# Five blocks of an output projection with other operand layouts: interleaved weights, 512 and 256 columns, another order of the three products, three PSUM banks

## The chip, the cores and the metric

The kernel runs on one core of one Trainium2 chip. The metric is the device time of one execution in microseconds (us); smaller is better. A profile is taken of one execution by the hardware profiler. The engines are called PE (TensorE, the matrix unit), PEld (its weight loads, which run under its matmuls), DVE (VectorE), ACT (ScalarE), POOL (GpSimd) and SP (SyncE, which here only starts transfers). SBUF is the working memory on the chip, PSUM the memory that matmuls write their sums to.

## The reference: what is computed

One layer of a streaming encoder, for 256 frames of a new stream and 64 frames of a running one, which share the weights. The kernel joins the two groups to T = 320 columns. Cut to what matters here:

```
proj = rmsnorm(x) @ w_in                    # q, k, v, u, v_s, gates
a  = stick_breaking_attention(q, k, v, cache)
bb = spatial_gate(gelu(u), rmsnorm(gelu(v_s)))
merged = g_a * (a @ w_branch_a) + g_b * (bb @ w_branch_b)
h = x + merged @ w_out                      # the output projection
gu = rmsnorm(h) @ w_gate_up
h = h + (silu(gu[:F]) * gu[F:]) @ w_down
y = rmsnorm(h)
```

The change concerns the line with `w_out`: a product of a 320 x 2048 activation with a 2048 x 2048 matrix, all in 32-bit floating point.

## The kernel before

Features lie on the 128 partitions, the 320 frames on the free dimension. A weight matrix is cut into blocks: one block makes 128 output features and has K / 128 tiles of 128 x 128 weights. For the output projection there are 16 blocks (`for m in range(KD)`, L660 to L666), and each sums over 16 values of k.

**Split operands.** TensorE's format fp32r keeps fewer bits than float32. So every operand is split into a high part (rounded to fp32r) and a low part (what the rounding left), and a product is three matmuls: high weights x high activation, high weights x low activation, low weights x high activation (`product`, L80 to L85). Each of them brings its 128 x 128 weights as a load of its own. For one block of the output projection these are 16 x 3 = 48 matmuls of 320 columns, all into one PSUM bank.

**Weights.** `weights` (L68 to L78) brings 8 tiles of weights, half a block, as one transfer of 512 KB on SP's queue into `raw` (three buffers), casts them on ACT to `wh` (L75) and subtracts on DVE to get `wl` (L76). `wh` and `wl` have four buffers each, so a cast for the half that comes four later waits until TensorE has used up the old one.

**The block.** `block` (L87 to L97) takes a PSUM accumulator `acc` (L45, three buffers of 512 columns, which is one bank), runs the two halves and returns the first 320 columns. The caller evicts: in the output projection DVE adds the residual x, which it has loaded to `xr` (L662), to the accumulator and writes h (L664); ACT and DVE then make the split, gain-scaled copy of h that the feed-forward part takes as its activation (L123, L124), and a sum of squares of h is kept (L197 on ACT, L198 mostly on POOL).

**The activation of the output projection** is `merged`, 16 pairs of tiles `mh` and `ml` (L651 to L655), 128 x 320 each, written at the end of each merge step.

**Order.** A scheduler decides the order of instructions on each engine, apart from those marked to be kept in program order. Small pieces of work of the attention are hung in between blocks by a counter of half blocks (`tick`); none falls into the output projection.

Other matmuls that the prediction uses as measures: L243 (the first blocks, fp32r, two heads at once in two PSUM banks), L416, L488 and L604 (attention and spatial gate, plain float32, 128 or 64 columns), L418 (attention, fp32r, 256 columns).

Of the kernel before, what the change touches and what calls it, by code (L numbers as in the profile page):

```python
# [8 lines left out]
F32 = mybir.dt.float32  # L9
F32R = mybir.dt.float32r  # L10
AF = mybir.ActivationFunctionType
ALU = mybir.AluOpType

P = 128
TP = 256
TS = 64
T = TP + TS
D = 2048
KD = D // P
H = 8  # L20
HALF = 8
# [12 lines left out]
def stream_step(ctx: ExitStack, tc: tile.TileContext, xT, w_in, w_a, w_b, w_out, w_gu, w_down,  # L34
                gains, ws_t, bs, ck_t, cv, y_t, k_t, v_t, sv_t):
    nc = tc.nc
    pool = lambda name, bufs=1, **kw: ctx.enter_context(tc.tile_pool(name=name, bufs=bufs, **kw))
    const = pool("const")
    wraw = pool("wraw", 3)
    wsplit = pool("wsplit", 4)  # L40
# [4 lines left out]
    def acc():  # L45
        return psum.tile([P, 512], F32, tag="acc", bufs=3, name="acc")

    def aux():
        return psum.tile([P, 512], F32, tag="aux", bufs=4, name="aux")

    def aux1():
        return psum.tile([P, 512], F32, tag="aux1", bufs=1, name="aux1")
# [9 lines left out]
    def tick():  # L62
        state["tick"] += 1
        for fn, a in later.pop(state["tick"], ()):
            fn(*a)


    def weights(src, n, view=lambda t: t):  # L68
        raw = wraw.tile([P, HALF * P], F32, tag="raw", name="raw")
        d = nc.sync.dma_start(out=view(raw[:, : n * P]), in_=src)  # L70
        if state["tick"] < 4:
            tc.keep_in_program_order(d)
        wh = wsplit.tile([P, HALF * P], F32R, tag="wh", name="wh")
        wl = wsplit.tile([P, HALF * P], F32R, tag="wl", name="wl")
        nc.scalar.copy(out=wh[:, : n * P], in_=raw[:, : n * P])  # L75
        nc.vector.tensor_tensor(out=wl[:, : n * P], in0=raw[:, : n * P],  # L76
                                in1=wh[:, : n * P].bitcast(F32), op=ALU.subtract)
        return wh, wl  # L78

    def product(ps, w, j, x, first, last):  # L80
        wh, wl = w
        a, b = wh[:, j * P : (j + 1) * P], wl[:, j * P : (j + 1) * P]
        nc.tensor.matmul(ps[:, :T], a, x[0], start=first, stop=False)  # L83
        nc.tensor.matmul(ps[:, :T], a, x[1], start=False, stop=False)  # L84
        nc.tensor.matmul(ps[:, :T], b, x[0], start=False, stop=last)  # L85

    def block(src, act):  # L87

        ps = acc()
        nk = len(act)  # L90
        for k0 in range(0, nk, HALF):
            n = min(HALF, nk - k0)
            w = weights(src[:, k0 * P : (k0 + n) * P], n)
            for j in range(n):
                product(ps, w, j, act[k0 + j], k0 + j == 0, k0 + j == nk - 1)
            tick()
        return ps[:, :T]  # L97

    def slot(tag):
        return big.tile([P, T], F32R, tag=tag, bufs=32, name=tag)  # L100
# [20 lines left out]
    def gained(tag, src, gain):  # L121
        hi, lo = slot(tag), slot(tag)
        nc.scalar.activation(out=hi, in_=src, func=AF.Copy, scale=gain)  # L123
        nc.vector.scalar_tensor_tensor(out=lo, in0=src, scalar=gain, in1=hi.bitcast(F32),  # L124
                                       op0=ALU.mult, op1=ALU.subtract)
        return hi, lo

    def t320(tag, bufs=2, dt=F32):
        return tmp.tile([P, T], dt, tag=tag, bufs=bufs, name=tag)
# [76 lines left out]
    first = [[acc(), acc()], [aux(), aux()], [aux(), aux()]]  # L206
# [340 lines left out]
    for h in range(2, H):  # L547
        if h % 2 == 0:
            att_new(h // 2)
            at(state["tick"] + 6, att_keys, h // 2)  # L550
            at(state["tick"] + 9, att_past, h // 2)
        for name, b in (("k", 1), ("q", 0), ("v", 2)):
            head_out(name, block(w_in[b * H + h], xs), h)
        if h % 2:
            att_parts(h // 2)
            attend(h // 2, state["tick"])
# [4 lines left out]
    for g in range(H):  # L561
        ps = block(w_in[4 * H + g], xs)
        t = t320("ev")
        nc.vector.tensor_tensor(out=t, in0=ps, in1=got["rx"], op=ALU.mult)
        nc.scalar.activation(out=vs[g], in_=t, func=AF.Gelu_apprx_tanh)
        sq.add(vs[g])
# [57 lines left out]
    for g in range(H):  # L624
        ps = block(w_in[3 * H + g], xs)
        t = t320("ev")
        nc.vector.tensor_tensor(out=t, in0=ps, in1=got["rx"], op=ALU.mult)
        nc.scalar.activation(out=us[g], in_=t, func=AF.Gelu_apprx_tanh)
# [3 lines left out]
    merged = []  # L632
    for m in range(KD):
        gate = []
        for i in range(2):
            ps = block(w_in[5 * H + i * KD + m], xs)
            t = t320("ev")
            nc.vector.tensor_tensor(out=t, in0=ps, in1=got["rx"], op=ALU.mult)
            gt = t320(f"gate{i}", 1)
            nc.scalar.activation(out=gt, in_=t, func=AF.Sigmoid, bias=b_gate[:, i * KD + m : i * KD + m + 1])  # L640
            gate.append(gt)
        if m == 0:
            att_ctx.close()
            mpool = mctx.enter_context(tc.tile_pool(name="merged", bufs=1))
        ps = block(w_a[m], [aT[h] for h in range(H)])
        t = t320("mg", 1)
        nc.vector.tensor_tensor(out=t, in0=ps, in1=gate[0], op=ALU.mult)
        ps = block(w_b[m], [bT[g] for g in range(H)])
        nc.vector.tensor_tensor(out=gate[1], in0=ps, in1=gate[1], op=ALU.mult)
        nc.vector.tensor_tensor(out=t, in0=t, in1=gate[1], op=ALU.add)  # L650
        hi = mpool.tile([P, T], F32R, tag="C", bufs=32, name="mh")  # L651
        lo = mpool.tile([P, T], F32R, tag="C", bufs=32, name="ml")
        nc.scalar.copy(out=hi, in_=t)
        nc.vector.tensor_tensor(out=lo, in0=t, in1=hi.bitcast(F32), op=ALU.subtract)
        merged.append((hi, lo))  # L655


    (hs, ypair), hg = halves(KD, "h"), []
# [1 line left out]
    for m in range(KD):  # L660
        x = t320("xr")
        tc.keep_in_program_order(nc.sync.dma_start(out=x, in_=xT[:, m, :]))  # L662
        ps = block(w_out[m], merged)
        nc.vector.tensor_tensor(out=hs[m], in0=ps, in1=x, op=ALU.add)  # L664
        hg.append(gained("A", hs[m], g_ffn[:, m : m + 1]))
        sq.add(hs[m], nc.vector if m == KD - 1 else None)  # L666
# [6 lines left out]
    last = const.tile([P, T], F32, name="last")  # L673
# [3 lines left out]
    for s0, n in SLICES:  # L677
        act = []
# [17 lines left out]
        for m in range(KD):  # L696
            ps = block(w_down[m][:, s0 * P : (s0 + n) * P], act)
# [20 lines left out]
    ps, cols = aux1(), aux()  # L718
    keep(nc.tensor.matmul(cols[:, 1:2], mones, tiny, start=True, stop=False, skip_group_check=True))
    for i, t in enumerate((sqf.total, last)):  # L720
        keep(nc.tensor.matmul(ps[:, inner], mones, t[:, inner], start=i == 0, stop=i == 1))  # L721
        for c, r in enumerate(COLS):
            keep(nc.tensor.matmul(cols[0 : r.stop - r.start, c : c + 1], t[:, r], mones[:, 0:1], start=False,
                                  stop=i == 1, skip_group_check=True))
# [4 lines left out]
    x, e = root[:, inner], half[:, inner]  # L729
# [10 lines left out]
    for c, r in enumerate(COLS):  # L740
        keep(nc.tensor.matmul(far[:, r], col[:, c : c + 1].to_broadcast([P, P]), ident[:, 0 : r.stop - r.start],
                              start=c == 0, stop=c == 1, skip_group_check=True))
# [83 lines left out]
```

## Time and profile before

| what | value |
|---|---|
| time, median of 3 runs | 1701.74 us (1701.65 to 1701.96) |
| span of the profiled execution | 1700.0 us |
| DVE busy | 881.0 us |
| ACT busy | 673.2 us |
| POOL busy | 58.4 us |
| DMA, mean over the span | 158 GB/s |
| output projection, first to last eviction | 653.0 to 758.6 us |
| mean granted TensorE clock | 0.998 |

The profiled execution's own time is its span, from the first to the last instruction; the runs are timed from outside and come out 1.74 us above it. A row of a group reads: line, engine, operation, output <- inputs, shape, count, busy time and mean length of one in ns, then the idle time of the engine ahead of it and what ended it. A row of the order in time begins with its start and its length in us. A row of the chain of work that ended last has start, length, engine, what is written, line and count. TensorE's ends are modelled by the profiler, so that neighbouring matmuls overlap in the rows; their starts are what can be measured.

### The profile page before, as it was taken

Reading aid. Unit: us, or ns where it says so; the run is one execution under the profiler, and the core shown is the slowest. Engines: PE = TensorE matmul, PEld = TensorE weight load, DVE = VectorE, ACT = ScalarE, POOL = GpSimd, SP = SyncE. Lnnn points to the kernel's source line nnn. Section 1 sums busy time; section 2 is a strip of 40 time slices with the busy share of each in tenths; the row PEclk is TensorE's granted clock in tenths of the full one; section 3 lists DMA queues with packets and bytes.
Section 4 is the critical chain, followed back from the end, with each engine's and each line's share of the span. In section 5 each row is a group of like instructions: output and inputs, shape, how many; then the busy total and the mean of one; then the engine's idle time right before and its main releaser. Section 6 shows DMA issues by size and latency. Waiting matters only on the chain.

```text
span 1700.0 us, 27477 instructions
## 1 busy us (share of the span) xinstructions
PE 1690.0 (99%) x11550; PEld 1689.2 (99%) x11550; DVE 881.0 (52%) x1150; ACT 673.2 (40%) x885; POOL 58.4 (3%) x81
## 2 busy tenths in 40 slices
PE   9999999999999999999999999999999999999997
PEld 9999999999999999999999999999999999999997
DVE  6677656544444445555444444444444444444455
ACT  6655545433333333443333332333333323333342
POOL 0300021000000000110000000000000000000000
PEclk9999999999999999999999999999999999999999
DMA  6676556544444455554444455444444554444453
GB/s 249 195 219 173 172 168 173 147 151 152 150 150 151 150 156 165 173 164 149 150 149 150 150 152 150 151 151 149 150 149 149 149 149 150 150 152 149 132 150 124
DMA packets 100507, 268.30 MB, mean 158 GB/s; under 512 B 28992, under 2 KB 35392, under 8 KB 100384
## 3 DMA queue, kind: packets, MB, share of 16 engines
q1 hardware_dynamic: 97936, 261.36, 49.8%
q0 software_dynamic: 1312, 3.80, 0.7%
q8 instruction: 90, 1.47, 0.4%
q10 hardware_dynamic: 1136, 1.39, 0.2%
q14 instruction: 33, 0.27, 0.0%
HBM read 256.03 MB, written 5.51 MB: 154 GB/s over the span
## 4 chain that ended last, share of the span: by engine, by line
PE 99%; DVE 0%; DMA 0%; ACT 0%; DVEq 0%; issue 0%
PE acc L84 32%; PE acc L83 32%; PE acc L85 32%; PE aux L243 2%; PE acc L243 1%; PE aux L488 1%; DVE h L749 0%; PE aux L604 0%; DMA gain<-gains 0%; PE aux L418 0%; PE aux L421 0%; PE aux L416 0%; PE aux L602 0%; PE aux L721 0%; ACT A L123 0%; ACT wh L233 0%
## 5 line engine op out<-in xcount | busy, mean ns | idle before, releaser
L75 ACT CAST wh<-raw 128x1024 fp32r<-128x1024 f32 x468 | 484.4, 1036 | 922.8 <-PE acc L84 746.6
L76 DVE TENSOR_TENSOR wl<-raw,wh 128x1024 fp32r<-128x1024 f32 x468 | 564.8, 1207 | 476.0 <-ACT wh L75 475.3
L83 PE MATMUL acc<-A,wh 128*128 128x320 f32 x2464 | 762.0, 309 | 0.0
L85 PE MATMUL acc<-A,wl 128*128 128x320 f32 x2464 | 761.4, 309 | 0.0
L84 PE MATMUL acc<-A,wh 128*128 128x320 f32 x2464 | 761.4, 309 | 0.0
L83 PEld LDWEIGHTS acc<-A,wh 128*128 128x128 f32 x2464 | 462.5, 188 | 0.0
L84 PEld LDWEIGHTS acc<-A,wh 128*128 128x128 f32 x2464 | 462.5, 188 | 0.0
L85 PEld LDWEIGHTS acc<-A,wl 128*128 128x128 f32 x2464 | 462.5, 188 | 0.0
L83 PE MATMUL acc<-B,wh 128*128 128x320 f32 x960 | 296.6, 309 | 0.0
L84 PE MATMUL acc<-B,wh 128*128 128x320 f32 x960 | 296.6, 309 | 0.0
L85 PE MATMUL acc<-B,wl 128*128 128x320 f32 x960 | 296.6, 309 | 0.0
L83 PEld LDWEIGHTS acc<-B,wh 128*128 128x128 f32 x960 | 180.2, 188 | 0.0
L84 PEld LDWEIGHTS acc<-B,wh 128*128 128x128 f32 x960 | 180.2, 188 | 0.0
L85 PEld LDWEIGHTS acc<-B,wl 128*128 128x128 f32 x960 | 180.2, 188 | 0.0
L83 PE MATMUL acc<-mh,wh 128*128 128x320 f32 x256 | 79.1, 309 | 0.0
L84 PE MATMUL acc<-ml,wh 128*128 128x320 f32 x256 | 79.1, 309 | 0.0
L85 PE MATMUL acc<-mh,wl 128*128 128x320 f32 x256 | 79.1, 309 | 0.0
L683 DVE TENSOR_TENSOR ev<-acc,rh 128x320 f32<-128x320 f32 x44 | 21.6, 492 | 56.6 <-PE acc L85 56.6
L686 DVE TENSOR_TENSOR bb<-acc,rh 128x320 f32<-128x320 f32 x44 | 21.6, 492 | 56.5 <-PE acc L85 56.5
L83 PEld LDWEIGHTS acc<-mh,wh 128*128 128x128 f32 x256 | 48.0, 188 | 0.0
L84 PEld LDWEIGHTS acc<-ml,wh 128*128 128x128 f32 x256 | 48.0, 188 | 0.0
L85 PEld LDWEIGHTS acc<-mh,wl 128*128 128x128 f32 x256 | 48.0, 188 | 0.0
(184 smaller groups left out, 732.5 us busy)
## 6 DMA issues: line engine op xcount, KB each, us to landing
raw<-w_gu SPq DMA_DIRECT2D x176, 512.0 KB, 3.6
raw<-w_in SPq DMA_DIRECT2D x141, 512.0 KB, 3.7
raw<-w_down SPq DMA_DIRECT2D x80, 512.0 KB, 3.6
raw<-w_out SPq DMA_DIRECT2D x32, 512.0 KB, 3.6
raw<-w_a SPq DMA_DIRECT2D x16, 512.0 KB, 3.6
raw<-w_b SPq DMA_DIRECT2D x16, 512.0 KB, 3.5
raw<-w_down SPq DMA_DIRECT2D x16, 256.0 KB, 2.6
x<-xT SPq DMA_DIRECT2D x8, 320.0 KB, 7.6
```

The costliest lines, as they stand in the source:

```text
L75: nc.scalar.copy(out=wh[:, : n * P], in_=raw[:, : n * P])
L76: nc.vector.tensor_tensor(out=wl[:, : n * P], in0=raw[:, : n * P], in1=wh[:, : n * P].bitcast(F32), op=ALU.subtract)
L83: nc.tensor.matmul(ps[:, :T], a, x[0], start=first, stop=False)
L84: nc.tensor.matmul(ps[:, :T], a, x[1], start=False, stop=False)
L85: nc.tensor.matmul(ps[:, :T], b, x[0], start=False, stop=last)
L243: nc.tensor.matmul(first[b][h][:, :T], w[:, (h * n + j) * P : (h * n + j + 1) * P], xs[c + j][i], start=not last and c + j + i == 0, stop= ...
L488: mm = lambda out, a, b, first, last: nc.tensor.matmul(out, a, b, start=first, stop=last, skip_group_check=True)
L683: nc.vector.tensor_tensor(out=t, in0=pg, in1=got["rh"], op=ALU.mult)
L686: nc.vector.tensor_tensor(out=u, in0=pu, in1=got["rh"], op=ALU.mult)
```

## The change

Blocks 2, 5, 8, 11 and 14 of the 16 get a function of their own; the other eleven keep `block`. All compute the same sums of three products.

- **Block 2, `woven`:** the high and low weights of a tile lie interleaved, word by word, in one buffer, so that a weight load reads every second 4-byte word. Each half block's cast and subtraction are made in two pieces of 512 columns.
- **Block 5, `wide`:** high and low activation lie side by side in 640 columns. High weights are multiplied with the first 512 of them in one matmul into one bank and with the other 128 in a second matmul into another bank; low weights with the 320 high columns into the first bank. `plus` then joins the pieces.
- **Block 8, `narrow`:** each of the three products is made for 256 columns (first group of frames) and for 64 columns (second group) apart, into two banks: six matmuls for each k.
- **Block 11, `ordered`:** the low weights come between the two uses of the high weights.
- **Block 14, `banks`:** each of the three products has a PSUM bank of its own, which `plus` joins.

`plus` copies the first bank to SBUF on ACT and adds the others on DVE; the residual addition then reads that copy. For all blocks the pairs `mh`, `ml` become one tile of 640 columns, `mhl`.

```diff
+    def tiles_of(src):
+        for k0 in range(0, KD, HALF):
+            w = weights(src[:, k0 * P : (k0 + HALF) * P], HALF)
+            for j in range(HALF):
+                yield k0 + j, w[0][:, j * P : (j + 1) * P], w[1][:, j * P : (j + 1) * P]
+            tick()
+    def plus(ps, more):
+        t = t320("ev")
+        nc.scalar.copy(out=t, in_=ps)
+        for r, src in more:
+            nc.vector.tensor_tensor(out=t[:, r], in0=src, in1=t[:, r], op=ALU.add)
+        return t
+    def woven(src, act):
+        ps = acc()
+        n = HALF * P // 2
+        for k0 in range(0, KD, HALF):
...
+            for i, tag in enumerate(("wh", "wl")):
+                t = wsplit.tile([P, HALF * P], F32R, tag=tag, name=tag).rearrange("p (n w) -> p n w", w=2)
+                nc.scalar.copy(out=t[:, :, 0], in_=raw[:, i * n : (i + 1) * n])
+                nc.vector.tensor_tensor(out=t[:, :, 1], in0=raw[:, i * n : (i + 1) * n],
+                                        in1=t[:, :, 0].bitcast(F32), op=ALU.subtract)
+                w.append(t)
+            for j in range(HALF):
+                a, b = (w[j // 4][:, j % 4 * P : (j % 4 + 1) * P, i] for i in range(2))
...
+    def wide(src, act):
+        ps, rest = acc(), acc()
+        for k, a, b in tiles_of(src):
+            mm(ps, a, act[k][:, :512], k == 0, False)
+            mm(rest[:, : 2 * T - 512], a, act[k][:, 512:], k == 0, k == KD - 1)
+            mm(ps[:, :T], b, act[k][:, :T], False, k == KD - 1)
+        return plus(ps[:, :T], ((slice(0, 512 - T), ps[:, T:]), (slice(512 - T, T), rest[:, : 2 * T - 512])))
+    def narrow(src, act):
+        ps, rest = acc(), acc()
+        for k, a, b in tiles_of(src):
+            for i, (w, o) in enumerate(((a, 0), (a, T), (b, 0))):
+                mm(ps[:, :TP], w, act[k][:, o : o + TP], k + i == 0, k + i == KD + 1)
+            for i, (w, o) in enumerate(((a, 0), (a, T), (b, 0))):
+                mm(rest[:, :TS], w, act[k][:, o + TP : o + T], k + i == 0, k + i == KD + 1)
...
+    def ordered(src, act):
...
+            mm(ps[:, :T], a, act[k][:, :T], k == 0, False)
+            mm(ps[:, :T], b, act[k][:, :T], False, False)
+            mm(ps[:, :T], a, act[k][:, T:], False, k == KD - 1)
+    def banks(src, act):
+        ps = acc(), acc(), aux()
+        for k, a, b in tiles_of(src):
+            for p, w, o in zip(ps, (a, a, b), (0, T, 0)):
+                mm(p[:, :T], w, act[k][:, o : o + T], k == 0, k == KD - 1)
+        return plus(ps[0][:, :T], [(slice(0, T), p[:, :T]) for p in ps[1:]])
...
-        ps = block(w_out[m], merged)
+        form = {2: woven, 5: wide, 8: narrow, 11: ordered, 14: banks}.get(m)
+        if form:
+            ps = form(w_out[m], merged)
+        else:
+            ps = block(w_out[m], [(t[:, :T], t[:, T:]) for t in merged])
```

In the changed kernel the lines behind `block` move down by 73: L664 becomes L741, L123 and L124 become L196 and L197, and the matmuls of the five functions all have the line of their helper, L106.

The order of the matmuls on TensorE at the start of block 5, two values of k, before the change (numbers tell buffers apart; `wh`, `wl` are the split weights):

```order
L83 MATMUL acc_7128<-mh_3760,wh_7131 128x320
L84 MATMUL acc_7128<-ml_3761,wh_7131 128x320
L85 MATMUL acc_7128<-mh_3760,wl_7132 128x320
L83 MATMUL acc_7128<-mh_3960,wh_7131 128x320
L84 MATMUL acc_7128<-ml_3961,wh_7131 128x320
L85 MATMUL acc_7128<-mh_3960,wl_7132 128x320
```

and at the same place of the change, block 5 again:

```order
L106 MATMUL acc_7116<-mhl_3760,wh_7120 128x512
L106 MATMUL acc_7117<-mhl_3760,wh_7120 128x128
L106 MATMUL acc_7116<-mhl_3760,wl_7121 128x320
L106 MATMUL acc_7116<-mhl_3959,wh_7120 128x512
L106 MATMUL acc_7117<-mhl_3959,wh_7120 128x128
L106 MATMUL acc_7116<-mhl_3959,wl_7121 128x320
```

The number of matmuls for one k stays at three; the widths and the banks change. At the start of block 8, the same engine of the changed kernel (x2: two matmuls one behind the other on the same tiles):

```order
L106 MATMUL acc_7334<-mhl_3760,wh_7338 128x256 x2
L106 MATMUL acc_7334<-mhl_3760,wl_7339 128x256
L106 MATMUL acc_7335<-mhl_3760,wh_7338 128x64 x2
L106 MATMUL acc_7335<-mhl_3760,wl_7339 128x64
L106 MATMUL acc_7334<-mhl_3959,wh_7338 128x256 x2
L106 MATMUL acc_7334<-mhl_3959,wl_7339 128x256
L106 MATMUL acc_7335<-mhl_3959,wh_7338 128x64 x2
L106 MATMUL acc_7335<-mhl_3959,wl_7339 128x64
```

Here one k has six matmuls where before it had three of 320 columns. At the end of block 5, on ScalarE, with the change (L75 casts the weights of later halves, L110 is the copy of `plus`, L196 the scaled copy of h, L270 its squares):

```order
L196 ACTIVATE A_7107<-h_6750,gain_76 128x320
L270 ACTIVATE sq_7111<-h_6750 128x320
L75 CAST wh_7266<-raw_7264 128x1024
L75 CAST wh_7296<-raw_7294 128x1024
L110 COPY ev_7178<-acc_7116 128x320
L196 ACTIVATE A_7183<-h_6750,gain_76 128x320
L270 ACTIVATE sq_7187<-h_6750 128x320
L75 CAST wh_7338<-raw_7336 128x1024
```

Only the copy is new in this row; before, the two casts are followed directly by the scaled copy of h.

More of the change, by code (lines that the diff above doesn't have):

```diff
@@ L97, in block @@
         return ps[:, :T]
+    def tiles_of(src):
[4 more added lines that the diff above has]
+            tick()
+    mm = lambda out, a, b, first, last: nc.tensor.matmul(out, a, b, start=first, stop=last, skip_group_check=True)
+    def plus(ps, more):
[4 more added lines that the diff above has]
+        return t
@@ new lines, in woven @@
+    def woven(src, act):
+        ps = acc()
+        n = HALF * P // 2
+        for k0 in range(0, KD, HALF):
+            raw = wraw.tile([P, HALF * P], F32, tag="raw", name="raw")
+            nc.sync.dma_start(out=raw, in_=src[:, k0 * P : (k0 + HALF) * P])
+            w = []
+            for i, tag in enumerate(("wh", "wl")):
[6 more added lines that the diff above has]
+                a, b = (w[j // 4][:, j % 4 * P : (j % 4 + 1) * P, i] for i in range(2))
+                x = act[k0 + j]
+                mm(ps[:, :T], a, x[:, :T], k0 + j == 0, False)
+                mm(ps[:, :T], a, x[:, T:], False, False)
+                mm(ps[:, :T], b, x[:, :T], False, k0 + j == KD - 1)
+            tick()
+        return ps[:, :T]
@@ new lines, in wide @@
+    def wide(src, act):
[12 more added lines that the diff above has]
+                mm(rest[:, :TS], w, act[k][:, o + TP : o + T], k + i == 0, k + i == KD + 1)
+        t = t320("ev")
+        nc.scalar.copy(out=t[:, :TP], in_=ps[:, :TP])
+        nc.scalar.copy(out=t[:, TP:], in_=rest[:, :TS])
+        return t
@@ new lines, in ordered @@
+    def ordered(src, act):
+        ps = acc()
+        for k, a, b in tiles_of(src):
+            mm(ps[:, :T], a, act[k][:, :T], k == 0, False)
+            mm(ps[:, :T], b, act[k][:, :T], False, False)
+            mm(ps[:, :T], a, act[k][:, T:], False, k == KD - 1)
+        return ps[:, :T]
+    def banks(src, act):
+        ps = acc(), acc(), aux()
+        for k, a, b in tiles_of(src):
+            for p, w, o in zip(ps, (a, a, b), (0, T, 0)):
+                mm(p[:, :T], w, act[k][:, o : o + T], k == 0, k == KD - 1)
+        return plus(ps[0][:, :T], [(slice(0, T), p[:, :T]) for p in ps[1:]])
@@ L650, in stream_step @@
         nc.vector.tensor_tensor(out=t, in0=t, in1=gate[1], op=ALU.add)
-        hi = mpool.tile([P, T], F32R, tag="C", bufs=32, name="mh")
-        lo = mpool.tile([P, T], F32R, tag="C", bufs=32, name="ml")
+        both = mpool.tile([P, 2 * T], F32R, tag="C", bufs=16, name="mhl")
+        hi, lo = both[:, :T], both[:, T:]
         nc.scalar.copy(out=hi, in_=t)
         nc.vector.tensor_tensor(out=lo, in0=t, in1=hi.bitcast(F32), op=ALU.subtract)
-        merged.append((hi, lo))
+        merged.append(both)
     (hs, ypair), hg = halves(KD, "h"), []
```

## The prediction

> **What bounds the kernel now.** First the page: the share of each engine, and the chain of work that ended last.
>
> ```profile
> span 1700.0 us, 27477 instructions
> ...
> PE 1690.0 (99%) x11550; PEld 1689.2 (99%) x11550; DVE 881.0 (52%) x1150; ACT 673.2 (40%) x885; POOL 58.4 (3%) x81
> ...
> PE 99%; DVE 0%; DMA 0%; ACT 0%; DVEq 0%; issue 0%
> ```
>
> The chain is TensorE from end to end; VectorE and ScalarE are about half idle. Busy time alone does not say that TensorE waits for nobody, since its rows overlap, so the second view is that of the waits, for TensorE alone. These two rows are its whole answer.
>
> ```profile
> PE aux L214 <- PEq L809: 0.8, 1, 0.8
> PE acc L243 <- ACT wh L233: 0.4, 1, 0.4
> ```
>
> Both lie in the first six us. In the rest, the output projection included, no wait of TensorE is recorded. So the time of a block is the number of its matmuls times the step from one to the next, and the change is priced by steps. The third view is the order in time of TensorE inside the output projection, and beside it the row of the 16 evictions, one at the end of each block.
>
> ```profile
> 715.72 0.31 PE L83 MATMUL acc<-mh,wh 128*128 128x320 f32 x1
> 715.87 0.31 PE L84 MATMUL acc<-ml,wh 128*128 128x320 f32 x1
> 716.02 0.31 PE L85 MATMUL acc<-mh,wl 128*128 128x320 f32 x1
> 716.16 0.31 PE L83 MATMUL acc<-mh,wh 128*128 128x320 f32 x1
> ...
> L664 DVE TENSOR_TENSOR h<-acc,xr x16: 491/492/492, 653.0 to 758.6; 128x320 f32<-128x320 f32 x16
> ```
>
> Each matmul is shown as 0.31 us long, but they start 0.147 us apart; the start counts. Fifteen blocks lie between the first and the last eviction: (758.6 - 653.0) / 15 = 7.04 us, and 48 matmuls x 0.147 = 7.04 us. The two agree, so a block holds no gap.
>
> What sets a step? The chain in order of time has matmuls of other widths (start, us, line, count), and the order in time has the weight loads (PEld), each of which runs under the matmul before its own.
>
> ```profile
> 41.06 7.04 PE aux L243 x48
> ...
> 62.18 0.22 PE aux L416 x2
> ...
> 99.35 0.36 PE aux L418 x3
> ...
> 115.02 1.00 PE L488 MATMUL aux<-wt,cv 128*128 128x64 f32 x8
> ...
> 114.91 0.97 PEld L488 LDWEIGHTS aux<-wt,cv 128*128 128x128 f32 x8
> 115.80 0.42 PEld L488 LDWEIGHTS aux<-B 128*128 128x128 f32 x3
> ...
> 279.15 0.89 PE aux L604 x8
> ...
> 279.77 0.19 PEld L83 LDWEIGHTS acc<-A,wh 128*128 128x128 f32 x1
> 279.88 0.19 PEld L84 LDWEIGHTS acc<-A,wh 128*128 128x128 f32 x1
> ```
>
> L418 is fp32r (tile B) with 256 columns: 0.36 / 3 = 0.120 us a step. From 256 to 320 columns a step thus grows by 0.027 us, 0.00042 us a column. By that slope 128 columns would take 0.066 us and 64 columns 0.040, but L604 (128 columns) steps by 0.89 / 8 = 0.111 and L488 (64 columns) by (115.80 - 114.91) / 8 = 0.111. Below about 230 columns the step no longer falls: it is the time of the 128-column weight load that each matmul brings with it. Those two lines are plain fp32; that an fp32r load takes as long is seen at 279.77, where the load of L83 starts under a short matmul and the next load starts 0.11 us later. So I take: **step = the larger of 0.111 us and 0.013 + 0.00042 x columns.**
>
> **The change part by part.** All five blocks keep 960 columns for each of the 16 values of k; what differs is how many loads these are cut into, and which lie under a matmul too short to hide them.
>
> Block 8 (256 and 64 columns): six matmuls for each k in place of three, three of 256 and three of 64 columns. 16 x (3 x 0.120 + 3 x 0.111) = 16 x 0.693 = 11.09 us against 7.04: **+4.05 us**.
>
> Block 5 (512, 128 and 320 columns): for 512 columns the trace has no row. By the slope it is 0.147 + 192 x 0.00042 = 0.227 us; if the step grew in proportion to the columns, 0.235, which is 0.1 us more for the block; I take the slope. 16 x (0.227 + 0.111 + 0.147) = 7.76 us: **+0.72 us**.
>
> Block 14 (three banks): the same 48 matmuls, each into another bank than the one before. L243, quoted above, goes to the other head's bank after every second matmul, for its low weights after every one, and its 48 take 7.04 us, the same 0.147 each: **0**. Block 11 (order hi, low weight, lo): every matmul has its own load already, L84 too, which repeats the weights of L83 (both have a load in the rows above), so another order saves none and adds none: **0**.
>
> Block 2 (weights at every second word): its matmuls stay at 320 columns and 0.147 us. Its loads read 128 words with a step of 8 bytes, which no row of the trace shows. From below the bound is 0, since the load is not what the step waits for and a faster one gains nothing. It has 0.147 - 0.111 = 0.036 us of cover, so it may become a third slower for nothing. If the step doubled it, it would be 0.222 us, and the block 48 x (0.222 - 0.147) = **+3.6 us**: the upper bound. Counting twice its bytes, the load would read 128 x 8 / 0.111 = 9.2 bytes per ns of a partition, where the moving operand already reads 320 x 4 / 0.147 = 8.7. That row is nearly there, so I take **0** and keep 3.6 for the range. The Trainium skill, "SBUF — State Buffer", Door 1: The DMA port swizzle, says that SBUF is read in 16-byte lines, at full rate with at least two hits in a line; a step of 8 bytes has just two, which would be 0 too, though it also charges each change of line. No run here shows a strided load.
>
> The other engines: block 2 cuts two casts and two subtractions into four of half the size each. Blocks 5, 8 and 14 put a ScalarE copy from PSUM, and blocks 5 and 14 two VectorE additions, ahead of the residual addition. The evictions of one block look so now:
>
> ```profile
> 695.10 1.05 ACT L75 CAST wh<-raw 128x1024 fp32r<-128x1024 f32 x1 [2.47 <-PE acc L84]
> 696.05 0.56 ACT L123 ACTIVATE A<-h,gain 128x320 fp32r<-128x320 f32 x1
> ...
> 695.24 0.49 DVE L664 TENSOR_TENSOR h<-acc,xr 128x320 f32<-128x320 f32 x1 [1.36 <-PE acc L85]
> 696.18 1.23 DVE L76 TENSOR_TENSOR wl<-raw,wh 128x1024 fp32r<-128x1024 f32 x1 [0.44 <-ACT wh L75]
> ...
> ACT wh L75 <- PE acc L84: 746.6, 343, 2.5
> ```
>
> The copy is about 0.56 us (as L123), an addition at most 0.49 (as L664): up to 1.5 us more before h is done, and the next cast and subtraction stand behind it in the queues of their engines. The cover: the casts wait for TensorE to free a weight buffer (343 times), so with four buffers three halves of a block, 3 x 3.52 = 10.6 us of matmuls, lie ready. A PSUM bank is wanted again 7 us later at the soonest: blocks 5, 8 and 14 take two of the three accumulators, the third was emptied a block earlier. In the new order the copy of block 5 stands behind a cast that waits for the same block's end, which adds 1.05 us, still far from 7. So **0**; without that cover it would be 1.5 us at each of three blocks, 4.4 us. The weight transfers on SyncE keep their number, and two move ahead of a load of x, which is wanted only at a block's end. GpSimd's order is unchanged, and the merged tiles that now hold both halves side by side fill the same bytes. The path after the projection begins with TensorE again.
>
> The sum: 4.05 + 0.72 = **+4.77 us** on the profiled span, 1704.8. The median of the runs, 1701.74, is 1.74 us over the span of 1700.0, which lies outside it and stays: **1706.5 us**, 0.28% slower.
>
> **The rivals.** A measurement of this kernel can tell about 0.2% from no change, 3.4 us. Let s be the step of the short matmuls (64 and 128 columns): the two blocks then change by 64 x s - 2.34 us.
>
> (a) **Not slower**: a short fp32r matmul is not held by its load, because loads run two ahead, say. Then s follows the columns, 0.040 and 0.066: 48 x 0.040 + 16 x 0.066 - 2.34 = +0.6 us, 1702.3. It decides from s below 0.090. For it speaks only that no fp32r matmul under 256 columns is in the trace; against it the 0.111 steps of L488, whose eight loads of different weights in a row were no faster, and the 0.11 of the fp32r load at 279.77. The Trainium skill, "TensorE: Matmul & The Clock Gate", Back-to-back issue gap, gives 81 ns for 128 columns and 131 ns for 512 as the sustained step; with these (81 for the short ones) the sum would be an estimated +1.3 us and no measurable change. The trace speaks against it: 320 columns already step by 147 ns.
>
> (b) **The strided load is slow**: +3.6 us beside the rest, 1710.1. No row speaks for it but the absence of one; the 0.036 us of cover and the byte rates above speak against it.
>
> (c) **Short fp32r matmuls run twice**, as each plain fp32 one does: the 16 of L604 in the source are 32 rows.
>
> ```profile
> L604 PE MATMUL aux<-wst,vsn x32: 275/275/275, 279.0 to 314.8; 128*128 128x128 f32 x32
> ```
>
> Then s = 0.222 and the sum is 64 x 0.222 - 2.34 = +11.9 us, 1713.6. Against it: fp32r at 256 and 320 columns runs once, and nothing in the trace ties that to the width.
>
> (d) **TensorE waits for an eviction or for weights** after the changed blocks: up to 4.4 us more, 1710.9. Against it stands the lead of 10.6 us.
>
> That the blocks are not built as described is no rival: the order of TensorE shows the new widths.
>
> **How the numbers follow.** Forecast 0.60; (b) 0.14; (c) 0.06; (d) 0.06; (a) 0.14, of which 0.02 for an end faster than before. Slower by over 0.2%: 0.60 + 0.14 + 0.06 + 0.06 = 0.86; within 0.2%: 0.12; faster: 0.02. The range leaves out (a) and (c), 0.20. Its low end is the forecast with the 256 and 64 column steps 0.015 us shorter on average (96 of them, 1.5 us), 1705.0; its high end takes in (b) and (d), 1711.0.
>
> **What would show it.** In the changed profile the evictions of the projection's blocks (L741) should lie 11.1 us apart at block 8, 7.8 at block 5 and 7.04 at blocks 2, 11 and 14. In block 8 the loads under 64 columns should start 0.111 us apart, those under 256 columns 0.120. If they start 0.04 apart, (a) holds; if 64 columns give two rows, (c). If block 2 is longer with no wait of TensorE, it is (b); if a wait of TensorE appears behind block 5, 8 or 14, it is (d). A time below 1705 or above 1711 makes the forecast wrong in its terms.

## The result, and the profile after

The changed kernel takes 1706.3 us (median; 1706.14 to 1706.55) against 1701.74 us before; the ratio is 1.0027, with a 95% interval of 1.0017 to 1.0037. It is slower by 4.6 us, where 4.77 us were forecast; the interval leaves 1.7 us of room to either side.

From the page of the changed kernel, these are the lines on the span, on the engines and on the chain that ended last. The row behind them is the whole answer to the question what TensorE waited for (PEq is its sequencer):

```profile
span 1704.4 us, 27591 instructions
...
PE 1694.8 (99%) x11598; PEld 1693.3 (99%) x11598; DVE 879.9 (52%) x1156; ACT 674.6 (40%) x891; POOL 57.2 (3%) x81
...
PE 99%; DVE 0%; ACT 0%; DVEq 0%; issue 0%
```

```profile
PE aux L287 <- PEq L886: 0.8, 1, 0.8
```

The changed blocks have brought no wait: TensorE is as continuous as before. It has 48 more matmuls, all in block 8. The span grew by 4.4 us, while the blocks below add up to 4.75. The first wait on ScalarE (0.4 us, in the first six us) is absent in this execution, and the projection starts 0.3 us sooner; it is absent in some other runs too. The chain in order of time (start, length, engine, tile, line, count) has each of the four blocks whose sums all lie in `acc` as one row, and block 14 as pairs, since its third bank is of `aux`:

```profile
659.65 7.04 PE acc L106 x48
680.77 7.79 PE acc L106 x48
702.64 10.96 PE acc L106 x96
713.60 0.23 PE acc L83
727.76 7.04 PE acc L106 x48
748.88 0.29 PE acc L106 x2
...
755.48 0.29 PE acc L106 x2
```

These are blocks 2, 5, 8, 11 and 14. Blocks 2 and 11 have the old 7.04 us; block 14 has (755.48 - 748.88) / 15 = 0.44 us for each k, which is 3 x 0.147. Block 5 is 0.75 us longer. Block 8 takes 10.96, and the first matmul behind it 0.23 in place of 0.15, since its load lay under a 64-column matmul: together 4.0 us more. The sum is 4.75 us.

The steps themselves are read from the starts of the weight loads: first in block 5, then in block 8 (the order in time of PEld; x2 means two loads in a row).

```profile
681.81 0.19 PEld L106 LDWEIGHTS acc<-mhl,wl 128*128 128x128 f32 x1
681.92 0.34 PEld L106 LDWEIGHTS acc<-mhl,wh 128*128 128x128 f32 x2
682.30 0.19 PEld L106 LDWEIGHTS acc<-mhl,wl 128*128 128x128 f32 x1
...
704.44 0.30 PEld L106 LDWEIGHTS acc<-mhl,wh 128*128 128x128 f32 x2
704.67 0.19 PEld L106 LDWEIGHTS acc<-mhl,wl 128*128 128x128 f32 x1
704.79 0.30 PEld L106 LDWEIGHTS acc<-mhl,wh 128*128 128x128 f32 x2
705.01 0.19 PEld L106 LDWEIGHTS acc<-mhl,wl 128*128 128x128 f32 x1
```

In block 5 the load of wl starts under the 128-column matmul, and the next load starts 0.11 us later, not 0.066; one k takes 682.30 - 681.81 = 0.49 us. In block 8 three loads take 0.33 to 0.35 us, so that the three 256-column and the three 64-column matmuls of a k take 0.69 us together. The short ones step at 0.11.

### The profile page after: what moved, and what is told of

The parts are those of the page before. It is cut to its first block, busy times and chain, and to the rows that moved or that the text cites. A ratio compares the mean times of both kernels' runs of the same rounds, so it can differ in the third digit from the quotient of the medians.

```text
span 1704.4 us, 27591 instructions
## 1 busy us (share of the span) xinstructions
PE 1694.8 (99%) x11598; PEld 1693.3 (99%) x11598; DVE 879.9 (52%) x1156; ACT 674.6 (40%) x891; POOL 57.2 (3%) x81
## 4 chain that ended last, share of the span: by engine, by line
PE 99%; DVE 0%; ACT 0%; DVEq 0%; issue 0%
PE acc L85 31%; PE acc L83 31%; PE acc L84 31%; PE acc L106 2%; PE aux L316 2%; PE acc L316 1%; PE aux L561 1%; DVE h L826 0%; PE aux L287 0%; PE aux L677 0%; PE aux L491 0%; PE aux L494 0%; PE aux L106 0%; PE aux L489 0%; PE aux L675 0%; PE aux L798 0%
## 5 line engine op out<-in xcount | busy, mean ns | idle before, releaser
L75 ACT CAST wh<-raw 128x1024 fp32r<-128x1024 f32 x466 | 482.2, 1036 | 909.0 <-PE acc L84 715.3
L83 PE MATMUL acc<-mhl,wh 128*128 128x320 f32 x176 | 54.5, 309 | 0.0
L85 PE MATMUL acc<-mhl,wl 128*128 128x320 f32 x176 | 54.4, 309 | 0.0
L84 PE MATMUL acc<-mhl,wh 128*128 128x320 f32 x176 | 54.4, 309 | 0.0
L781 DVE TENSOR_TENSOR h<-acc,h 128x320 f32<-128x320 f32 x47 | 23.0, 489 | 46.4 <-PE acc L85 46.4
L711 DVE TENSOR_TENSOR ev<-acc,rx 128x320 f32<-128x320 f32 x32 | 15.7, 492 | 42.0 <-PE acc L85 42.0
L106 PE MATMUL acc<-mhl,wh 128*128 128x320 f32 (+4 forms) x184 | 36.3, 297 | 0.0
```

What stands on the lines that cost most here:

```text
L106: mm = lambda out, a, b, first, last: nc.tensor.matmul(out, a, b, start=first, stop=last, skip_group_check=True)
L781: nc.vector.tensor_tensor(out=hs[m], in0=ps, in1=hs[m], op=ALU.add)
```

## The experiments

The first theory is that a step is the larger of a fixed time of the load and a time that grows with the columns. Its rivals are short matmuls that run free of their loads (a), a slow strided load (b), short fp32r matmuls that run twice (c) and lost cover (d). Times of a block below are from its first load to the first load of the next block, as the traces have them; rows of the chain count from the matmuls and can differ by 0.1 us.

**One form in all blocks.** Block 8's form sixteen times makes its term large against the measurement; the same for block 2's form; and the change without block 8.

```diff
-        form = {2: woven, 5: wide, 8: narrow, 11: ordered, 14: banks}.get(m)
+        form = narrow                                                  # e1, with rest = aux()
+        form = {2: woven, 5: wide, 11: ordered, 14: banks}.get(m)      # e2
+        form = woven                                                   # e3
```

> All 16 blocks of the output projection with the 256 and 64 columns of block 8; the 64-column sums go to the other PSUM pool. If short matmuls are held at 0.111 us by their loads, each block is 16 x (3 x 0.120 + 3 x 0.111) = 11.1 us, 4.0 more than before, and the run 64 us longer than before (1766, ratio 1.038). If they followed their columns (0.039 us), 0.6 a block, 9.5 us in all. If they ran twice (0.222), 9.4 a block, 150 us.

> The change without block 8's part; blocks 2, 5, 11 and 14 as changed. If the widths alone make the time, 0.74 us over before (ratio 1.0004, not to be told from no change). If block 8 was longer only in company with the others, or the layout of the merged tiles cost something, more than that stays: up to 4.6.

> All 16 blocks with weights at every second word, everything else as in block. If the strided load stays under its matmul, every block keeps 7.04 us and the run is as before (1701.7). If it were a little over its cover of 0.036 us somewhere, 16 blocks show 16 times of it; at double length it would be 58 us. If the four smaller casts and subtractions used up the lead of the weights, TensorE would wait, which the waits would show.

Measured: e1 1765.89 us, ratio 1.0376 (1.0361 to 1.0390), 64.1 us more, each block 11.04 us. e2 1702.48 us, ratio 1.0004 (0.9995 to 1.0012). e3 1701.74 us, ratio 0.9999 (0.9990 to 1.0008). The chain of e3 has its sixteen blocks as one piece:

```profile
645.87 112.64 PE acc L106 x768
```

112.64 / 768 = 0.1467 us a matmul: neither the strided loads nor the smaller casts cost anything sixteen times over. e1 rules out (a) and (c) for the 64 columns. e2 leaves block 8 as nearly the whole of the change, and shows that the joined tiles of the other eleven blocks are free.

**What makes the floor: the load's length.** Block 8 alone, with loads of half the columns under its short matmuls.

```diff
+                m_ = P if k == 0 else P // 2
-                mm(rest[:, :TS], w, act[k][:, o + TP : o + T], ...)
+                mm(rest[:m_, :TS], w[:, :m_], act[k][:, o + TP : o + T], ...)
```

> Block 8 alone as in the change, but from the second k on the 64-column matmuls take 64 of their 128 output features, so that their loads have 64 columns (the upper 64 features of the second frame group stay incomplete in this block). Two of the three short steps of each k then have a load of 64 columns under them, the third still the 128 columns of the next wide matmul. If the load's length sets the short step, two steps of 15 k fall from 0.111 to about 0.056: block 8 takes 11.07 - 15 x 2 x 0.055 = 9.4 us. If a floor of the matmul itself (issue, or fp32r at few columns) sets it, 11.07 us stays.

Block 8 took 9.45 us, where it takes 11.07 in the change. The order in time of its loads:

```profile
704.71 0.30 PEld L106 LDWEIGHTS acc<-mhl,wh 128*128 128x128 f32 x2
704.94 0.19 PEld L106 LDWEIGHTS acc<-mhl,wl 128*128 128x128 f32 x1
705.06 0.25 PEld L106 LDWEIGHTS acc<-mhl,wh 128*64 128x64 f32 x2
705.23 0.14 PEld L106 LDWEIGHTS acc<-mhl,wl 128*64 128x64 f32 x1
705.29 0.30 PEld L106 LDWEIGHTS acc<-mhl,wh 128*128 128x128 f32 x2
```

The wl load of 64 columns starts at 705.23, and the one behind it 0.06 us later, where 128 columns keep 0.11. All three short matmuls of a k write 64 features, but only two of their steps fell: one k takes 705.29 - 704.71 = 0.58 us, which is 3 x 0.12 + 0.11 + 2 x 0.056, and with all three shorter it would be 0.53. The step that stayed is the one with the 128-column load of the next k under it. So the floor is the load, 0.87 ns for each of its columns (0.111 / 128), and no floor of the matmul: shown.

**Where the floor ends.** Cuts of the 320 columns of each product (e6), and of the 640 joined columns (e7).

```diff
+        form = {1: cut(160), 3: cut(192), 5: cut(224), 7: cut(240), 9: cut(288)}.get(m)        # e6
+        form = {2: both_cut(384), 5: both_cut(400), 8: both_cut(448), 11: both_cut(512)}.get(m)  # e7
+    # cut: as narrow, [:c] into acc and [c:320] into aux; both_cut: as wide, [:c] and [c:640], rest = aux()
```

> Five blocks whose 320 columns are cut in two at 160, 192, 224, 240 and 288, six matmuls for each k. By the larger of 0.111 us and 0.013 + 0.00042 x columns: 160 + 160, 192 + 128 and 224 + 96 all 96 x 0.111 = 10.66 us a block; 240 + 80 10.8; 288 + 32 16 x 3 x (0.134 + 0.111) = 11.8 (before 7.04). If fp32r under 256 columns went slower by the column (a fixed multiple), the blocks would differ by their widths, and 160 + 160 would be the longest. If short matmuls followed their columns, all would be near 7.6.

> Blocks 2, 5, 8 and 11 multiply the high weights with the 640 joined columns cut at 384, 400, 448 and 512, the second piece into the other PSUM pool. If only a piece under its load's 0.111 us costs anything: 384 + 256 7.04 us (0 more), 400 + 240 7.06, 448 + 192 7.3, 512 + 128 7.78. If a wide matmul, the crossing from the high into the low half, or the second bank itself cost something, the first two would be longer than 7.04 as well.

e6: the blocks cut at 160, 192 and 224 took 10.75 us each, at 240 10.77, at 288 11.76. Three different cuts with one time are the mark of a floor: the columns do not matter as long as both pieces lie under it. At 240 columns the block is 0.02 us longer: the floor ends about there. The loads of the block cut at 160 start 0.11 us apart throughout:

```profile
655.89 0.19 PEld L106 LDWEIGHTS acc<-mhl,wh 128*128 128x128 f32 x1
656.00 0.19 PEld L106 LDWEIGHTS acc<-mhl,wl 128*128 128x128 f32 x1
656.11 0.30 PEld L106 LDWEIGHTS aux<-mhl,wh 128*128 128x128 f32 x2
656.34 0.19 PEld L106 LDWEIGHTS aux<-mhl,wl 128*128 128x128 f32 x1
```

e7: 7.04, 7.00, 7.31 and 7.78 us for 384, 400, 448 and 512. So neither 512 columns, nor the second bank, nor the crossing into the low half costs anything by itself; the short remainder does. The 7.00 was not expected, and is taken up below.

**Strided loads by themselves.** Under 64 columns a load has no cover. e4 puts interleaved weights there, and e9 other distances under 320 columns.

```diff
+    # tiles_woven(src, step): high and low weights of step / 2 tile groups interleaved, a load reads every step-th word
+        form = {2: woven4, 5: narrow2, 8: narrow, 11: narrow4}.get(m)     # e4: step 4 under 320; 2, 1, 4 in narrow's form
+        form = {2: woven3, 6: woven8, 10: woven4}.get(m)                  # e9: steps 3, 8, 4 under 320
```

> Block 8 as in the change; block 5 the same 256 and 64 columns with weights at every second word; block 11 the same with weights at every fourth word (16 bytes); block 2 with every fourth word under 320 columns. Under 64 columns the load has no cover, so the step there is the load's own time. If a load takes one step a word whatever the distance, 0.111 us in all three and 11.07 us for blocks 5, 8 and 11, 7.04 for block 2. If it pays for bytes or lines, 0.222 at every second word (block 5: 3 x 16 x 0.111 = 5.3 us more, and its 256-column steps 0.222 too, 4.9 more) and 0.444 at every fourth word, where block 2 would take 48 x 0.444 = 21 us.

> Weights at every third word in block 2, at every eighth in block 6, at every fourth in block 10, all under 320 columns; the other blocks as before. The last run gave 0.117 to 0.120 us a load at every second word and 0.233 at every fourth. If a load pays for each 16-byte line that it opens (four, two, 4/3, one word a line), the third word costs about 0.233 x 3/4 = 0.175 us, so block 2 takes 48 x 0.175 = 8.4 us, and from the fourth word on nothing more is lost: blocks 6 and 10 both 11.2 us. If it pays by the distance, the third word gives again 0.175, but the eighth doubles to 0.466, and block 6 takes 22 us.

The run of e4 took 1731.09 us beside 1701.78. Its chain, blocks 2, 5, 8 and 11 (the first lines), and that of e9, blocks 2, 6 and 10:

```profile
660.20 11.20 PE acc L106 x48
685.49 11.32 PE acc L106 x96
710.97 10.96 PE acc L106 x96
736.09 22.48 PE acc L106 x96
```

```profile
659.81 8.37 PE acc L106 x48
689.30 11.56 PE acc L106 x48
721.98 11.20 PE acc L106 x48
```

Neither run records a wait of TensorE in these blocks. At every second word the 96 steps are 11.32 / 96 = 0.118 us on average, at every fourth 22.48 / 96 = 0.234; both of e4's expectations missed. e9 separates their successors: 8.37 / 48 = 0.174 us at every third word, 0.241 at every eighth, 0.233 at every fourth. So the price hardly grows with the distance once a line holds one word. The Trainium skill, "SBUF — State Buffer", Door 1: The DMA port swizzle, says that SBUF is read in 16-byte lines and that each access that crosses to a new line pays. The runs agree: a step of four words opens 128 lines and takes 0.233 us, so 1.82 ns a line. By that price the 96 lines of a step of three would take 0.175 us (0.174 measured) and the 64 lines of a step of two 0.117 (0.118 measured); for the 32 lines of contiguous weights it gives an estimated 0.058, below the 0.111 that their columns take. A step of two words therefore costs 0.007 us of the 0.036 us of cover, and that is why block 2 is free.

**A bank wanted too soon.** (d) had to be provoked: block 6 in block 5's form too.

```diff
+        form = {2: woven, 5: wide, 6: wide, 8: narrow, 11: ordered, 14: banks}.get(m)   # e8
+        form = {2: woven, 5: kept, 6: kept, 8: narrow, 11: ordered, 14: banks}.get(m)   # e10: wide, each matmul kept in program order
```

> The change, with block 6 made as block 5 is: two neighbours that take two of the three accumulators each, so that block 6 needs a bank of block 5 at its second matmul. If a bank is free only after the cast ahead of the copy, the copy and the first addition, TensorE waits about 1.05 + 0.5 + 0.35 = 1.9 us at the start of block 6, on VectorE or ScalarE; blocks 5 and 6 together are 2 x 0.74 + 1.9 us longer than before. If the evictions have more cover than I think, no wait, 2 x 0.74.

> The last but one kernel again, blocks 5 and 6 both in the form of block 5, but with their matmuls kept in program order, since the scheduler had put seven of block 6's 128-column matmuls off and so avoided the wait. Now the second matmul of block 6 needs the bank that VectorE empties only after a cast (1.05 us), a subtraction (1.23) and its first addition (about 0.4): TensorE should wait about 2.4 us there, blocks 5 and 6 take 2 x 7.78 + 2.4 = 18.0 us together. If the bank came free sooner than that, or if the three accumulators were enough, 15.6 us.

In e8 blocks 5 and 6 took 7.79 and 7.92 us, with no wait: a miss, because the scheduler had put seven of block 6's 128-column matmuls off until the bank was free. In e10 they took 18.07 us together, 2.5 more than twice 7.78. The trace shows a wait there (the row of TensorE's waits, then the order in time of ACT, DVE and PE); its 2.2 us count from the modelled end of the matmul before:

```profile
PE acc L106 <- DVE ev L112: 2.2, 1, 2.2
```

```profile
688.74 1.04 ACT L75 CAST wh<-raw 128x1024 fp32r<-128x1024 f32 x1 [2.84 <-PE acc L106]
689.70 0.42 ACT L110 COPY ev<-acc 128x320 f32<-128x320 f32 x1
689.82 1.23 DVE L76 TENSOR_TENSOR wl<-raw,wh 128x1024 fp32r<-128x1024 f32 x1 [2.66 <-ACT wh L75]
690.96 0.55 DVE L112 TENSOR_TENSOR ev<-acc,ev 128x192 f32<-128x192 f32 x2
...
691.37 0.33 PE L106 MATMUL acc<-mhl,wh 128*128 128x128 f32 x1 [2.23 <-DVE ev L112]
```

The copy and the first addition take 0.42 us and about 0.4; most of the wait is a cast and a subtraction of weights that stand ahead of them in their queues. In the change itself the banks are wanted 7 us later, so the price exists and is not paid.

**A cut that gains.** The 7.00 us of e7 was looked at in eight cuts (e11), and the best was used widely (e12).

```diff
+        form = {1: both_cut(336), 3: both_cut(360), 5: both_cut(376), 7: both_cut(392),
+                9: both_cut(400), 11: both_cut(408), 13: both_cut(416), 15: both_cut(432)}.get(m)   # e11
+    # e12: in block(), from the second merge step on and where act has 16 joined pairs (A tiles too are one of 640 columns)
+            mm(ps[:, :400], a, both[:, :400], k == 0, False)
+            mm(rest[:, :240], a, both[:, 400:], k == 0, k == KD - 1)
+            mm(ps[:, :T], b, both[:, :T], False, k == KD - 1)
```

> The odd blocks multiply the high weights with the 640 joined columns cut at 336, 360, 376, 392, 400, 408, 416 and 432 (block 1 to block 15), the even ones are as before. An earlier run had 14.03 us instead of 14.08 for the block cut at 400 and its neighbour. By the larger of 0.111 us and 0.013 + 0.00042 x columns every cut up to 400 costs nothing and gains nothing (14.08 for a block and the next), and 408, 416 and 432 cost 0.01, 0.08 and 0.2 us. If the 0.013 us a matmul is instead something that another cut avoids in part, the cuts near 400 show 14.03 again or less, 3 ns for each k; a kernel that used it in some 136 blocks of 16 k would be 6 us shorter.

> The kernel before, with the 640 joined columns cut at 400 in 134 of its blocks of 16 k: the gates from the second on, all of the output projection and the gate-up blocks; each is joined by a ScalarE copy and two VectorE additions. Two runs have shown 14.03 us instead of 14.08 for one such block and its neighbour. If that is a property of the cut, 134 x 0.047 = 6.3 us less than before (1695.5, ratio 0.9963). If it belongs to that place alone, or the three instructions for each block use up the lead of the weights or hold a PSUM bank too long, no gain or a loss with waits of TensorE.

In e11 each block with the one behind it took 14.18, 14.12, 14.08, 14.08, 14.03, 14.15, 14.28 and 14.29 us, in the order of the cuts: only 400 gains (14.08 is the time before). The rule of the prediction misses here on both sides: the cuts at 336 and 360 should have cost nothing and cost 0.10 and 0.04 us, those at 408 and 416 0.07 and 0.20 in place of 0.01 and 0.08. e12 takes **1695.0 us, ratio 0.9959 (0.9946 to 0.9973)**, 6.7 us less than before, where 6.3 were expected, and the fastest of all; its 134 blocks take 6.99 us each. TensorE's waits are again two, of 0.8 and 0.5 us, at the start. The loads in order of time, and the group of the joining additions:

```profile
700.00 0.19 PEld L123 LDWEIGHTS acc<-mhl,wh 128*128 128x128 f32 x1
700.14 0.19 PEld L123 LDWEIGHTS aux<-mhl,wh 128*128 128x128 f32 x1
700.32 0.19 PEld L123 LDWEIGHTS acc<-mhl,wl 128*128 128x128 f32 x1
700.43 0.19 PEld L123 LDWEIGHTS acc<-mhl,wh 128*128 128x128 f32 x1
```

```profile
L99 DVE TENSOR_TENSOR jn<-aux,jn 128x240 f32<-128x240 f32 x134 | 53.4, 399 | 0.0
```

One k takes 0.43 to 0.44 us; the 240 columns step at 0.11, just at the floor, where the rule of the prediction gave 0.114. The 53.4 us of the larger addition, and the copies beside it, are hidden in VectorE's and ScalarE's idle time. Why 400 + 240 is cheaper and none of the neighbouring cuts is stays open.

## Why the prediction was right

- **Block 8, +4.05 us:** 4.0 measured, and 4.0 in each of e1's sixteen. The floor of 0.111 us had been read from plain float32 matmuls and one fp32r load; e5 shows that it is the load. The 0.05 us that is missing lies in the 256-column step: 11.04 / 16 = 0.690 = 3 x 0.119 + 3 x 0.111, where 0.120 had been read.
- **Block 5, +0.72 us:** 0.75 measured. The 512 columns had no row; by e7 the penalty comes from the 128-column rest alone. By the linear rule 512 columns are 0.227 us; measured, 7.78 / 16 - 0.111 - 0.147 = 0.228. The rule had been drawn from two widths 64 columns apart, so that it holds to 0.001 us 192 columns further on is in part luck; e11 shows misses of up to 0.12 us a block for cuts between.
- **Block 2, 0:** right, and the reason given, the rate of bytes, was near it, though untested until e4 and e9. At the 8.7 bytes per ns that it took from the moving operand, 128 x 8 bytes take 0.118 us, which is the load that e4 measured, and 16 bytes in 1.82 ns are nearly the same rate, 8.8. What it lacked is that whole lines are paid: by bytes every eighth word would cost 0.47 us, and e9 has 0.241. The upper bound of 3.6 us took a doubled load; every fourth word, which does double it, costs 11.20 - 7.04 = 4.2.
- **Blocks 11 and 14, 0:** 7.04 us each. Here a load came with every matmul in either order, and changing banks cost nothing.
- **The other engines, 0:** no new wait. e10 puts the price of lost cover at 2.5 us for one place; the 1.5 us taken for it left out the cast and the subtraction of weights queued ahead of the copy and the addition (the prediction had the cast, but only within the cover).
- **Rivals (a) and (c)** fell by e1 and e6, (b) by e3, (d) by the waits of the changed kernel.

## What to carry to other kernels

Where TensorE is continuous, price a new layout by steps: for each matmul the larger of the time of its columns and of the weight load that lies under it, which is the next matmul's. Look for pieces so narrow that this load no longer hides; here the limit lay at about 240 columns. For interleaved stationary operands, count the 16-byte lines that a load opens and compare with the matmul above it: under 320 columns (0.147 us) two words were free (0.118), three were not (0.174). When two neighbouring blocks take more banks than are free, read what stands ahead of the eviction in its queue, since here that made most of the wait.

## What was not expected of the hardware

**The clock fell without a wait.** In e4's block 11 TensorE had no recorded wait and shows as 100% busy, but its 64- and 256-column matmuls stood behind loads of 0.234 us. The busy times by stretch, with the granted clock third from the end:

```profile
736.00:740.00 4.00, 4.00 (x19) 4.00 (x19) 2.79 (x3) 1.86 (x3) 1.07 (x1) 1.00 0.73 202
740.00:745.00 5.00, 5.00 (x22) 5.00 (x23) 0.00 (x0) 1.05 (x1) 0.00 (x0) 0.53 0.27 95
745.00:750.00 5.00, 5.00 (x24) 5.00 (x23) 1.22 (x1) 0.00 (x0) 0.00 (x0) 0.50 0.04 10
```

The clock is halved some 4 us into the block, and the next block's matmuls of 320 columns start at 0.27 us each before they return to 0.15 (the chain of e4):

```profile
759.79 0.27 PE acc L84
...
761.33 0.15 PE acc L85
```

That block takes 8.11 us in place of 7.04. Block 2 of e4 has the same loads of 0.233 us, but under 320 columns, and kept the full clock:

```profile
660.00:671.00 11.00, 11.00 (x49) 11.00 (x48) 4.02 (x4) 3.97 (x5) 1.07 (x1) 1.00 0.50 157
```

Both blocks stream 960 columns for each k, block 2 in 11.20 / 16 = 0.70 us and block 11 in 22.48 / 16 = 1.4, so block 11 fed the array half as densely. That this made the clock fall is argued from these two blocks of one execution; no run varies it. The Trainium skill, "TensorE: Matmul & The Clock Gate", Part 1: The HAM clock gate, describes a clock that is halved when the array has been idle for a window of about 3.4 us; here no idle time was recorded, and the clock was halved all the same. The loads themselves took the 0.233 us of block 2 in block 11 at half clock too: a load of every fourth word did not follow that clock.
